# The first ten microseconds of an encoder layer: the norm's gain spread by TensorE, a new order of loads, casts and transposes

## The chip, the core and the metric

The kernel runs on one core of a Trainium2 chip. Its time is the device time of one execution in microseconds (us); the profile shows one execution, instruction by instruction. The engines are PE (TensorE), ACT (ScalarE), DVE (VectorE), POOL (GpSimd) and SP, which here only issues transfers. Each works through its own queue in order, and they wait for each other by semaphores.

## The reference

One residual layer on x, 1024 tokens of 1024 float32 numbers. Cut to what matters here:

```python
def rmsnorm(x, g):
    xf = x.astype(jnp.float32)
    y = xf * lax.rsqrt(jnp.mean(xf * xf, axis=-1, keepdims=True) + EPS)
    return (y * g.astype(jnp.float32)).astype(x.dtype)
...
h = rmsnorm(x, g_mix[l])
z = h @ w_in[l]                      # pooling channels | q | k | v
...                                  # pooling mixer and differential attention
gates = jax.nn.sigmoid(h @ w_gate[l] + b_gate[l])
merged = gates[..., :D] * (y_pool @ w_branch_pool[l]) + gates[..., D:] * (y_attn @ w_branch_attn[l])
x = x + merged @ w_out[l]
h2 = rmsnorm(x, g_ffn[l])
x = x + jnp.square(jax.nn.relu(h2 @ w_up[l])) @ w_down[l]
```

## The kernel before

Tokens lie in eight tiles x0 to x7 of 128 rows. Products are made in float32 by three matmuls (`mm3`, L123): each operand is split into a high part, rounded to the fast float32r, and a low part, the rest; hi times hi, hi times lo and lo times hi are summed in PSUM. `split` (L118) makes the parts: ACT casts the high one, DVE or POOL subtracts it for the low one.

`norm_transpose` (L262) turns a tile of x into normalised, transposed, split operands hT: a sum of squares by ACT (`ss`; for x0 ACT and DVE take half each), the factor rs by DVE and a power on POOL (L260, L275), hn = x * rs * g on DVE in two halves (L281), eight 128x128 transposes on PE into two PSUM banks hps (L286), then four casts and four subtractions to hT, one pair for each of four pieces of the depth (kp 0 to 3). g must lie in all 128 partitions: `gmb` is loaded by one DMA that reads the row 128 times (L370).

The weights of head 0 come in four pieces w0 to w3, each two DMAs of 192 KB into `rqkv` (L334) and two splits into `wqkv` (L354). `stage_qkv` multiplies: for a tile t, z is summed over eight k, and k = 2 kp and 2 kp + 1 use piece kp of hT and of the weights (L439). The string START sets the order of this opening; a token "xN" loads a tile, "nN" normalises it, "wN" loads a weight piece, "sN" splits it, and an "s" with a letter behind takes POOL for the low half instead of DVE. NX says at which step of the loop over head and tile the other tiles are normalised.

What each engine's queue looks like is decided by a scheduler that takes the instructions in the order of writing as priority and places each where its own timing model has it ready. It does so over the whole program, so a change at the start can move instructions far behind it.

Behind the opening come eight heads of attention, with the gate products and the pooling mixer as filling between them, then the projections, and an MLP whose two products are made of seven half-size products each (a Strassen-Winograd scheme): in `up_pair` (L1054), X, Y, Z and W are banks, A.. and AS1 to AS4 the split weight sides, B.. and BT1 to BT4 the split token sides, U2 and U3 copies of bank X between the products that are added to it, z5 a copy of Z.

Of the kernel before, what the change touches and what calls it, by code (L numbers as in the profile page):

```python
# [41 lines left out]

START = "x0 g n0 w0 w1 w2u w3u x1 s0p s1 x2 s2p s3 x3"
NX = [-2, -1, 0, 0, 0, 1, 2, 3]
LX = [-2, -2, -2, -2, 0, 0, 1, 1]
# [12 lines left out]
def encoder_kernel(  # L58
# [41 lines left out]

    hcount = [0]

    def htile(shape, dt, name, th):
# [14 lines left out]
    def split(hi, lo, src, lo_eng=None):  # L118

        nc.scalar.copy(hi, src)  # L120
        (lo_eng or nc.vector).tensor_tensor(lo, src, f(hi), op=ALU.subtract)  # L121

    def mm3(ps, lhs_hi, lhs_lo, rhs_hi, rhs_lo, first, last, more=False):  # L123

        kw = {"skip_group_check": True} if more else {}
        nc.tensor.matmul(ps, lhs_hi, rhs_hi, start=first, stop=False, **kw)  # L126
        nc.tensor.matmul(ps, lhs_hi, rhs_lo, start=False, stop=False, **kw)  # L127
        nc.tensor.matmul(ps, lhs_lo, rhs_hi, start=False, stop=last, **kw)  # L128

# [132 lines left out]
    def norm_transpose(xt, gb, t, dst, hn, small, banks, halves=False):  # L262
# [16 lines left out]
        for j in range(2):  # L279
            js = slice(j * 512, (j + 1) * 512)  # L280
            nc.vector.scalar_tensor_tensor(hn[:, js], xt[:, js], rs, gb[:, js], op0=ALU.mult, op1=ALU.mult)  # L281
            trp, trtag = banks[j % len(banks)]
# [17 lines left out]
    with ExitStack() as ph:  # L300
# [8 lines left out]

        xs = {}  # L310

# [8 lines left out]
        def load_x(t):  # L320
            xs[t] = ut([P, D], F32, f"x{t}")
            for c in range(0, D, 512 if t == 0 else D):
                e = c + 512 if t == 0 else D
                nc.sync.dma_start(xs[t][:, c:e], x[t * P : (t + 1) * P, c:e])

# [14 lines left out]
        def norm_x(t):  # L340
# [18 lines left out]
        for w in START.split():  # L359
            if w[0] == "x":  # L360
                load_x(int(w[1]))
            elif w[0] == "n":
                norm_x(int(w[1]))
            elif w[0] == "w":
                load_w(0, int(w[1]), utf if w[2:] else raw)
            elif w[0] == "s":
                split_w(0, int(w[1]), nc.gpsimd if w[2:] else nc.vector)
            elif w[0] == "g":
                gmb = ut([P, D], F32, "gmb")
                nc.sync.dma_start(gmb, g_mix[0].partition_broadcast(P))  # L370


        rows = sp.tile([32, P], F32, name="rows")
        nc.gpsimd.memset(rows, 0.0)
        nc.sync.dma_start(rows[0:16, :], b_gate[0].rearrange("(r p) -> r p", p=P))
# [6 lines left out]
        lqk = s1([P, 4, HD], F32, "lqk", "oq")  # L382
        nc.sync.dma_start(lqk, lambda_qk[0].partition_broadcast(P))

        dist = s1([P, S], F32, "dist", "dist")
# [44 lines left out]
        def stage_qkv(h, t):  # L430
# [4 lines left out]
            for k in range(NK):  # L435
                l_hi = hT[k // 2, th, 0][:, k % 2, c0 : c0 + P]
                l_lo = hT[k // 2, th, 1][:, k % 2, c0 : c0 + P]
                w = Wh[h][k]
                mm3(z[:, 0:384], l_hi, l_lo, w[:, 0, :], w[:, 1, :], k == 0, k == NK - 1)  # L439
                yield  # L440
# [191 lines left out]
        def stage(w, g):  # L632
# [19 lines left out]
            elif w == "W" and t == 0 and h:  # L652
                for kp in range(NK // 2):
                    load_w(h, kp)
                    split_w(h, kp, nc.gpsimd)

        for g in range(-2, N + 8):
# [3 lines left out]
            for t in range(1, NT):  # L661
                if NX[t] == g:
                    norm_x(t)
            if g == G_DIST:
# [103 lines left out]
    gate_units = gates()  # L768
    for _ in range(G_FIRST):
        next(gate_units)  # L770
# [565 lines left out]
```

## Time and profile before

| | |
|---|---|
| median of 3 runs | 1549.46 us (1548.1 to 1549.97) |
| the profiled execution | 1548.34 us |
| its span, first to last instruction | 1546.6 us |
| PE busy | 1526.0 us, 99% |
| DVE, ACT, POOL busy | 1012.4, 816.5, 350.9 us |
| first instruction on PE | 8.94 us |

A row of the timeline reads: start, duration (both us), engine, line of the kernel, operation, output<-input, partitions x elements, count; in brackets the idle time of the engine ahead of it and what ended that. "SPq" rows are issues of DMAs, not their transfers.

### The profile page before, as it was taken

The numbers are of one execution on the slowest core, as the hardware profiler recorded it, in microseconds if no ns is written. First come the engines' busy times: TensorE is split into PE (matmuls) and PEld (weight loads), VectorE is DVE, ScalarE is ACT, GpSimd is POOL, SyncE is SP. The second block draws the span as 40 slices with busy tenths as digits, with TensorE's granted clock in tenths as the row PEclk, the third lists the DMA queues.
The fourth block names the chain that finished last, engine by engine and source line by source line (L and its number), as shares of the span: only waits on it lengthen the run. The fifth ranks groups of instructions, "written<-read, shape, count | busy, mean of one in ns | idle before, by whom it ended". The sixth has DMA issues, their size and how long they took to land.

```text
span 1546.6 us, 22053 instructions
## 1 busy us (share of the span) xinstructions
PE 1526.0 (99%) x7649; PEld 1320.4 (85%) x7649; DVE 1012.4 (65%) x2268; ACT 816.5 (53%) x1808; POOL 350.9 (23%) x448
## 2 busy tenths in 40 slices
PE   7999999999999999999999999999999999999999
PEld 6899999999998989888888887888888788888887
DVE  7777777777878787865322448766666668556672
ACT  6656555666666565566432546565555634333331
POOL 6433334243525262315443400000000000000000
PEclk9999999999999999999999999999999999999999
DMA  7111212020202031547426534555432789537650
GB/s 230 49 54 48 64 39 73 20 79 32 81 28 84 28 96 42 177 132 250 139 93 205 177 105 124 180 172 176 137 136 109 259 312 389 196 123 256 225 192 28
DMA packets 166681, 206.41 MB, mean 133 GB/s; under 512 B 10069, under 2 KB 102954, under 8 KB 166570
## 3 DMA queue, kind: packets, MB, share of 16 engines
q1 hardware_dynamic: 149162, 177.71, 34.8%
q10 hardware_dynamic: 17408, 27.30, 4.7%
q8 instruction: 60, 0.98, 0.3%
q14 instruction: 51, 0.42, 0.1%
HBM read 150.42 MB, written 54.56 MB: 133 GB/s over the span
## 4 chain that ended last, share of the span: by engine, by line
PE 91%; DVE 3%; issue 2%; ACT 1%; DMA 1%; POOL 1%; SPq 1%; POOLq 0%; DVEq 0%; ACTq 0%
PE z L126 5%; PE z L128 5%; PE z L127 5%; PE Da L126 4%; PE Da L127 4%; PE Da L128 4%; PE g L126 3%; PE g L127 3%; PE g L128 3%; PE Db L126 3%; PE Db L127 3%; PE Db L128 3%; PE X L126 2%; PE X L128 2%; PE X L127 2%; PE sc L512 2%
## 5 line engine op out<-in xcount | busy, mean ns | idle before, releaser
L126 PE MATMUL z<-wqkv,hT 128*128 128x384 f32 x512 | 174.5, 341 | 0.4 <-DVE qn L453 0.3
L128 PE MATMUL z<-wqkv,hT 128*128 128x384 f32 x512 | 174.1, 340 | 0.0
L127 PE MATMUL z<-wqkv,hT 128*128 128x384 f32 x512 | 173.8, 339 | 0.0
L522 ACT ACTIVATE s<-s,nm 128x256 f32<-128x256 f32 (+7 forms) x128 | 99.6, 778 | 45.8 <-DVE nm L514 42.7
L260 POOL TENSOR_TENSOR ms<-ms,mhalf 128x4 f32<-128x4 f32 x64 | 66.5, 1039 | 158.0 <-DVE ms L259 136.7
L126 PE MATMUL g<-hT,fwgate 128*128 128x512 f32 x256 | 101.0, 395 | 0.1
L127 PE MATMUL g<-hT,fwgate 128*128 128x512 f32 x256 | 101.0, 395 | 0.0
L128 PE MATMUL g<-hT,fwgate 128*128 128x512 f32 x256 | 101.0, 395 | 0.0
L126 PEld LDWEIGHTS z<-wqkv,hT 128*128 128x128 f32 x512 | 96.8, 189 | 3.9 <-DVE qn L453 1.0
L127 PEld LDWEIGHTS z<-wqkv,hT 128*128 128x128 f32 x512 | 96.6, 189 | 3.0
L128 PEld LDWEIGHTS z<-wqkv,hT 128*128 128x128 f32 x512 | 96.6, 189 | 2.2 <-DVE hT L121 0.5
L514 DVE CUSTOM_DVE_ANT_0 s<-sc,dist 128x512 f32<-128x512 f32 (+3 forms) x128 | 74.7, 586 | 19.7 <-PE sc L512 18.2
L121 POOL TENSOR_TENSOR wqkv<-rqkv,wqkv 128x384 fp32r<-128x384 f32 x60 | 64.0, 1085 | 19.2 <-ACT wqkv L120 15.5
L121 DVE TENSOR_TENSOR AS<-s,AS 128x512 fp32r<-128x512 f32 x64 | 43.9, 688 | 35.8 <-ACT AS L120 35.6
L511 PE MATMUL sc<-K,Q 128*128 128x512 f32 (+2 forms) x192 | 66.6, 353 | 0.1
L512 PE MATMUL sc<-K,Q 128*128 128x512 f32 (+2 forms) x192 | 66.5, 354 | 0.0
L459 POOL TENSOR_TENSOR qn<-qn,ggh 128x128 f32<-128x128 f32 x64 | 32.3, 505 | 138.7 <-DVE qn L453 127.7
L485 ACT CAST Q<-tk 64x128 fp32r<-64x128 f32 x128 | 33.2, 259 | 57.8 <-DVE Q L484 56.0
L482 ACT CAST Q<-tk 64x128 fp32r<-64x128 f32 x128 | 33.0, 258 | 53.7 <-DVE K L481 52.3
L121 POOL TENSOR_TENSOR fwgate<-frgate,fwgate 128x512 fp32r<-128x512 f32 x32 | 44.5, 1394 | 51.9 <-ACT fwgate L120 51.8
L128 PEld LDWEIGHTS g<-hT,fwgate 128*128 128x128 f32 x256 | 48.1, 188 | 8.6
L126 PEld LDWEIGHTS g<-hT,fwgate 128*128 128x128 f32 x256 | 48.2, 188 | 7.3 <-ACT go L757 0.4
(430 smaller groups left out, 4640.7 us busy)
## 6 DMA issues: line engine op xcount, KB each, us to landing
wd<-in_w_down_dram SPq DMA_DIRECT2D x56, 512.0 KB, 5.3
wu<-in_w_up_dram SPq DMA_DIRECT2D x32, 512.0 KB, 4.5
udS<-us SPq DMA_DIRECT2D x64, 256.0 KB, 2.4
ur<-udS SPq DMA_DIRECT2D x32, 512.0 KB, 3.3
rqkv<-in_w_in_dram SPq DMA_DIRECT2D x64, 192.0 KB, 2.7
ud<-u ACTq DMA_DIRECT2D x48, 256.0 KB, 2.1
ur<-ud SPq DMA_DIRECT2D x24, 512.0 KB, 4.7
frgate<-in_w_gate_dram SPq DMA_DIRECT2D x32, 256.0 KB, 2.6
```

Of the source, the lines that this page charges most:

```text
L121: (lo_eng or nc.vector).tensor_tensor(lo, src, f(hi), op=ALU.subtract)
L126: nc.tensor.matmul(ps, lhs_hi, rhs_hi, start=first, stop=False, **kw)
L127: nc.tensor.matmul(ps, lhs_hi, rhs_lo, start=False, stop=False, **kw)
L128: nc.tensor.matmul(ps, lhs_lo, rhs_hi, start=False, stop=last, **kw)
L260: nc.gpsimd.tensor_tensor(dst, dst, mhalf[:, :n], op=ALU.pow)
L459: nc.gpsimd.tensor_tensor(qn[:, 2:4, :], qn[:, 2:4, :], ggh.unsqueeze(1).broadcast_to([P, 2, HD]), op=ALU.mult)
L482: nc.scalar.copy(q_hi, q)
L485: nc.scalar.copy(Q[other, m, 1, :], q)
L511: nc.tensor.matmul(dst, Q[:, i, 0, :], rhs, start=True, stop=False)
L512: nc.tensor.matmul(dst, Q[:, i, 1, :], rhs, start=False, stop=True)
L514: nc.vector.tensor_tensor_reduce(out=s[i][:, c : c + w], in0=sc[:, 0:w], in1=dist[:, o0 + c : o0 + c + w], scale=2.0 ** -(h + 1), scalar=B ...
L522: nc.scalar.activation(s[i][:, 0:n], s[i][:, 0:n], AF.Exp, bias=last, scale=-1.0, accum_out=Z[:, i, t : t + 1])
```

## The change

The gain g is loaded as one row of 4 KB by ACT's DMA queue; two matmuls with a row of ones spread it over 128 partitions into two PSUM banks (g_ps), from which hn of x0 is made directly. DVE copies the banks to gmb for the other tiles, behind the first low half of hT. All other loads stay on SP: x0, w0, w1, x1, w2, w3, then the other tiles; the small parameters are held behind the last of the first x loads, as are the weights of head 1 and the first gate weights. The splits of w1, w2, w3 are held behind the first cast of hT, and the low halves of w0, w1 and w2 are made by POOL, those of w3 by DVE (before: w0 and w2 by POOL, w1 and w3 by DVE). x1 is normalised behind the whole first product, and x2 to x5 are normalised from step 1 on.

```diff
-START = "x0 g n0 w0 w1 w2u w3u x1 s0p s1 x2 s2p s3 x3"
-NX = [-2, -1, 0, 0, 0, 1, 2, 3]
+START = "x0 g n0 w0 w1 x1 w2u w3u s0p s1p s2p x2 s3 x3"
+NX = [-2, 1, 1, 1, 1, 1, 2, 3]
...
-            nc.vector.scalar_tensor_tensor(hn[:, js], xt[:, js], rs, gb[:, js], op0=ALU.mult, op1=ALU.mult)
+            nc.vector.scalar_tensor_tensor(hn[:, js], xt[:, js], rs, gb[j], op0=ALU.mult, op1=ALU.mult)
...
+                if kp == 0:
+                    marks["hT"], marks["hTl"] = marks["hi"], marks["lo"]
...
-            norm_transpose(xs.pop(t), gmb, t, hT, hn, sp, banks, t == 0)
+            gb = g_ps if t == 0 else [gmb[:, 0:512], gmb[:, 512:D]]
+            norm_transpose(xs.pop(t), gb, t, hT, hn, sp, banks, t == 0)
+            if t == 0:
+                with tc.issue_after(marks["hTl"]):
+                    for j in range(2):
+                        nc.vector.tensor_copy(gmb[:, j * 512 : (j + 1) * 512], g_ps[j])
...
             elif w[0] == "s":
-                split_w(0, int(w[1]), nc.gpsimd if w[2:] else nc.vector)
+                with ExitStack() as behind:
+                    if w[1] != "0":
+                        behind.enter_context(tc.issue_after(marks["hT"]))
+                    split_w(0, int(w[1]), nc.gpsimd if w[2:] else nc.vector)
             elif w[0] == "g":
                 gmb = ut([P, D], F32, "gmb")
-                nc.sync.dma_start(gmb, g_mix[0].partition_broadcast(P))
+                g_row = ut([1, D], F32, "g_row")
+                issued["g"] = nc.scalar.dma_start(g_row, g_mix).ins
+                g_ps = [pool.tile([P, 512], F32, tag=tag, name=f"g_ps{tag}") for pool, tag in ((ps_o, "o"), (ps_f, "f"))]
+                for j, ps in enumerate(g_ps):
+                    nc.tensor.matmul(ps, f(ones)[0:1, :], g_row[:, j * 512 : (j + 1) * 512], start=True, stop=True)
...
+                    with ExitStack() as behind:
+                        if t == 1:
+                            behind.enter_context(tc.issue_after(marks["z"]))
+                        norm_x(t)
```

POOL's queue at the start, before: the factor of x0, the low halves of the first and third weight piece (`wqkv0_4` is k = 4, piece 2), then the factors of x1 and x2.

```order
L275 TENSOR_TENSOR rs0_157<-rs0_157,mhalf_98 128x1
L121 TENSOR_TENSOR wqkv0_0_197<-rqkv0_0_183,wqkv0_0_197 128x384
L121 TENSOR_TENSOR wqkv0_1_200<-rqkv0_0_183,wqkv0_1_200 128x384
L121 TENSOR_TENSOR wqkv0_4_211<-rqkv0_2_189,wqkv0_4_211 128x384
L121 TENSOR_TENSOR wqkv0_5_214<-rqkv0_2_189,wqkv0_5_214 128x384
L260 TENSOR_TENSOR rs1_247<-rs1_247,mhalf_98 128x1
```

The same place now:

```order
L276 TENSOR_TENSOR rs0_162<-rs0_162,mhalf_98 128x1
L122 TENSOR_TENSOR wqkv0_0_204<-rqkv0_0_190,wqkv0_0_204 128x384
L122 TENSOR_TENSOR wqkv0_1_207<-rqkv0_0_190,wqkv0_1_207 128x384
L122 TENSOR_TENSOR wqkv0_2_210<-rqkv0_1_193,wqkv0_2_210 128x384
L122 TENSOR_TENSOR wqkv0_3_213<-rqkv0_1_193,wqkv0_3_213 128x384
L261 TENSOR_TENSOR rs1_295<-rs1_295,mhalf_98 128x1
L122 TENSOR_TENSOR wqkv0_4_216<-rqkv0_2_198,wqkv0_4_216 128x384
L122 TENSOR_TENSOR wqkv0_5_219<-rqkv0_2_198,wqkv0_5_219 128x384
```

The second piece's two halves came in between, and the third piece's now stand behind the factor of x1.

ACT's queue around the end of the first product z0_0, before (hn1, hn2, ... are the squares of x1, x2, ...; hps1_0 and hps1_1 the transposed halves of x1; sq0_0 and V0_0 read the product):

```order
L277 ACTIVATE hn2_275,ss2_276<-x2_209 128x1024
L448 ACTIVATE sq0_0_428<-z0_0_369 128x256
L120 CAST hT0_0_0_147<-hps1_0_252 128x2x128
L120 CAST hT2_0_0_151<-hps1_1_262 128x2x128
L277 ACTIVATE hn3_301,ss3_302<-x3_223 128x1024
L120 CAST hT1_0_0_149<-hps1_0_252 128x2x128
L277 ACTIVATE hn4_335,ss4_336<-x4_271 128x1024
L120 CAST V0_0_365<-z0_0_369 128x128
```

And now:

```order
L278 ACTIVATE hn2_319,ss2_320<-x2_222 128x1024
L468 ACTIVATE sq0_0_435<-z0_0_264 128x256
L121 CAST hT0_0_0_152<-hps1_0_300 128x2x128
L121 CAST hT2_0_0_156<-hps1_1_310 128x2x128
L278 ACTIVATE hn3_345,ss3_346<-x3_230 128x1024
L426 ACTIVATE ls_245<-ls_245 128x2
L278 ACTIVATE hn4_379,ss4_380<-x4_252 128x1024
L121 CAST V0_0_260<-z0_0_264 128x128
L121 CAST hT1_0_0_154<-hps1_0_300 128x2x128
```

The cast of the second piece of x1 (hT1) moved behind ls, the squares of x4 and V.

From about the 130th matmul, and the 50th instruction of the other queues, both programs agree, up to one stretch at the start of the MLP, where some 50 instructions of PE, ACT and DVE are permuted. There, ACT's queue before (u11_3, AS3_0 and A22_0 belong to different pairs of columns, 3 and 0):

```order
L120 CAST BT4h_10414<-y7_10307 128x4x128
L120 CAST AS3_0_10848<-s3_0_10808 128x512
L120 CAST A22_0_10871<-wu0_1_10629 128x512
L120 CAST AS4_0_10892<-s4_0_10809 128x512
L1094 COPY U2_0_10827<-X0_10590 128x512
L1099 COPY z5_0_10845<-Z0_10829 128x512
L1074 ACTIVATE u11_3_10777<-u11_3_10777 128x512
```

And now:

```order
L121 CAST BT4h_10421<-y7_10314 128x4x128
L1102 ACTIVATE u11_3_10784<-u11_3_10784 128x512
L1103 ACTIVATE u11_3_10784<-u11_3_10784 128x512
L1107 DMA ud11_1_10424<-u11_3_10784 128x512
L1122 COPY U2_0_10834<-X0_10597 128x512
L1127 COPY z5_0_10852<-Z0_10836 128x512
L121 CAST AS3_0_10855<-s3_0_10815 128x512
L121 CAST A22_0_10878<-wu0_1_10636 128x512
```

The copies of X0 and Z0 now stand ahead of the casts. On PE, the second product added to X0 (with AS3) before came behind the end of Y3 and the twelve matmuls of W0; now it follows the product with AS2 at once:

```order
L129 MATMUL X0_10597<-BT2h_10413,AS2_0_10819 128x512
L127 MATMUL X0_10597<-BT3h_10417,AS3_0_10855 128x512
L128 MATMUL X0_10597<-BT3l_10418,AS3_0_10855 128x512
L127 MATMUL W0_10877<-BT4h_10421,A22_0_10878 128x512
L128 MATMUL W0_10877<-BT4l_10422,A22_0_10878 128x512
```

W0's first two matmuls stand inside that product, its other ten behind the next one's start.

More of the change, by code (lines that the diff above doesn't have):

```diff
@@ L101, in encoder_kernel @@
     hcount = [0]
+    marks = {}
     def htile(shape, dt, name, th):
@@ L127, in mm3 @@
         nc.tensor.matmul(ps, lhs_hi, rhs_lo, start=False, stop=False, **kw)
-        nc.tensor.matmul(ps, lhs_lo, rhs_hi, start=False, stop=last, **kw)
+        return nc.tensor.matmul(ps, lhs_lo, rhs_hi, start=False, stop=last, **kw).ins
     wcount = [0]
@@ L308, in s1 @@
             return sq_pool.tile(shape, dt, tag=tag, name=name, bufs=bufs)
-        xs = {}
+        xs, issued = {}, {}
         def utf(shape, name):
@@ L383, in encoder_kernel @@
         nc.sync.dma_start(lqk, lambda_qk[0].partition_broadcast(P))
+        late.close()
         dist = s1([P, S], F32, "dist", "dist")
@@ L653, in stage @@
                 for kp in range(NK // 2):
-                    load_w(h, kp)
+                    with ExitStack() as behind:
+                        if h == 1:
+                            behind.enter_context(tc.issue_after(started))
+                        load_w(h, kp)
                     split_w(h, kp, nc.gpsimd)
@@ L662, in encoder_kernel @@
                 if NX[t] == g:
-                    norm_x(t)
+                    with ExitStack() as behind:
+                        if t == 1:
+                            behind.enter_context(tc.issue_after(marks["z"]))
+                        norm_x(t)
             if g == G_DIST:
@@ L768, in encoder_kernel @@
     gate_units = gates()
-    for _ in range(G_FIRST):
+    with tc.issue_after(started):
+        next(gate_units)
+    for _ in range(G_FIRST - 1):
         next(gate_units)
```

16 lines of the change are left out of this document (10 added, 6 removed).

## The prediction

> **What bounds the kernel now.** I read the page first, then the waits of TensorE, then the first 30 us of the timeline engine by engine, and last the stretch near 957 us, the only other place where the new order differs.
>
> ```profile
> span 1546.6 us, 22053 instructions
> PE 1526.0 (99%) x7649; PEld 1320.4 (85%) x7649; DVE 1012.4 (65%) x2268; ACT 816.5 (53%) x1808; POOL 350.9 (23%) x448
> PE hps L286 <- DVE hn L281: 9.6, 2, 8.9
> ```
>
> TensorE is busy for all but 20.6 us of the span, and 9.6 of those are two waits for the normalised row hn, 8.9 of them before its first instruction. Every later stage is a TensorE queue that the other engines keep fed, so what the change gains or loses ahead of the point where both orders meet is simply carried to the end. The profiled execution took 1548.34 us, the median is 1549.46; I sum against the first and add the result to the second. The three times shown span 1.9 us, and about 0.2% (3.1 us) is what a measurement of this kernel can tell from no change.
>
> How the first 9 us are made:
>
> ```profile
> 0.73 1.28 ACT L269 ACT_TABLE_LOAD   x1 [0.73 <-PEq L1322]
> 0.74 0.87 SPq L324 DMA_DIRECT2D x<-in_x_dram  x2
> 1.65 0.42 SPq L370 DMA_DIRECT2D gmb<-in_g_mix_dram  x1
> 2.12 6.96 SPq L334 DMA_DIRECT2D rqkv<-in_w_in_dram  x8
> 3.41 0.63 ACT L269 ACTIVATE hn<-x 128x512 f32<-128x512 f32 x1 [1.39 <-DMA x<-in_x_dram]
> 5.29 0.56 POOL L275 TENSOR_TENSOR rs<-rs,mhalf 128x1 f32<-128x1 f32 x1 [3.03 <-DVE rs L274]
> 8.13 1.41 DVE L281 SCALAR_TENSOR_TENSOR hn<-x,rs,gmb 128x512 f32<-128x512 f32 x2 [3.00 <-DMA gmb<-in_g_mix_dram]
> 8.94 1.97 PE L286 MATMUL hps<-identf,hn 128*128 128x128 f32 x8 [8.94 <-DVE hn L281]
> ```
>
> The row factor rs is ready at 5.29 + 0.56 = 5.85, yet hn starts at 8.13: the broadcast load of g ends that wait. The weights are queued behind it on SP.
>
> **Term 1: the first transposes.** The load of 128 copies of g is replaced by one row on ACT's queue and two matmuls. The row's issue stands ahead of the table load, which ended at 2.01 while ACT waited until 3.41, so it costs nothing with 1.4 us of cover. I let the row land no later than the first half of x0, which is 64 times its size and was used at 3.41. The two matmuls are of a kind the trace lacks (fp32, not a transpose, 512 columns). From below:
>
> ```profile
> 10.59 0.69 PE L126 MATMUL z<-wqkv,hT 128*128 128x384 f32 x1
> 13.01 0.52 PE L127 MATMUL z<-wqkv,hT 128*128 128x384 f32 x1
> 13.33 0.47 PE L128 MATMUL z<-wqkv,hT 128*128 128x384 f32 x1
> 13.64 0.34 PE L126 MATMUL z<-wqkv,hT 128*128 128x384 f32 x1
> 13.82 0.34 PE L127 MATMUL z<-wqkv,hT 128*128 128x384 f32 x1
> ```
>
> 384 columns step by 0.32 us (13.01 to 13.33), so 512 cost 0.43; from above, the eight fp32 transposes of 128 columns take 10.59 - 8.94 = 1.65, or 0.21 each, so 512 cost 0.83. I take the second, the nearer in type: both banks are there at 3.41 + 1.66 = 5.1, before rs. Then hn starts at 5.9 instead of 8.13 and the transposes at 6.65 instead of 8.94: **2.3 us earlier**. [...]
>
> The loads, too, must be there:
>
> ```profile
> 10.00:20.00 10.00, 9.37 (x47) 8.08 (x45) 8.39 (x20) 8.07 (x20) 6.91 (x9) 1.00 0.95 318
> ```
>
> The last number is GB/s. At 318, from 3.41 on, the other half of x0 and piece 0 (0.66 MB) take 2.1 us, piece 1 and x1 (0.92 MB) 2.9 more: piece 0 is there at 5.5, x1 at 8.4, each before it is wanted below (5.85 and 10.1).
>
> The two copies of g into gmb on VectorE (by the 0.70 of an hn half, at most 1.4 us) stand where two weight subtractions stood, and lie under POOL's next step.
>
> **Term 2: the first product waits for POOL.** The change hands POOL the low halves of weight piece 1, too: six subtractions instead of four, with rs1 behind the fourth. Their prices:
>
> ```profile
> 9.21 5.09 POOL L121 TENSOR_TENSOR wqkv<-rqkv,wqkv 128x384 fp32r<-128x384 f32 x4 [3.36 <-DMA rqkv<-in_w_in_dram]
> L121 POOL TENSOR_TENSOR wqkv<-rqkv,wqkv x60: 1001/1019/1497, 9.2 to 553.9; 128x384 fp32r<-128x384 f32 x60
> 10.43 0.98 ACT L120 CAST wqkv<-rqkv 128x384 fp32r<-128x384 f32 x2
> 19.66 0.36 ACT L120 CAST hT<-hps 128x256 fp32r<-128x256 f32 x1
> 18.61 1.06 ACT L277 ACTIVATE hn<-x 128x1024 f32<-128x1024 f32 x1
> ```
>
> At this place one took 5.09 / 4 = 1.27; the best of all 60 took 1.00. With 1.27: piece 0 is done at 5.85 + 2.54 = 8.4. Piece 1's casts stand on ACT behind the first hT cast, which four transposes (0.83) release near 7.6; so hT ends at 8.0, the casts (0.49 each) at 8.5 and 9.0, POOL's fourth at 8.5 + 2.54 = 11.0. ACT goes on with three hT casts (to 10.1) and the squares of x1, 1.05 with their sum, to 11.3 with the hand-over; VectorE's step and rs1 (0.56) end near 12.1. Piece 2 follows on POOL: 12.1 + 2.54 = 14.65. From there the first product lacks eight matmuls at 0.18: it ends near 16.05. Before:
>
> ```profile
> 16.11 0.34 PE L128 MATMUL z<-wqkv,hT 128*128 128x384 f32 x1
> 16.54 0.36 ACT L448 ACTIVATE sq<-z 128x256 f32<-128x256 f32 x1
> 17.07 1.23 PE L286 MATMUL hps<-identf,hn 128*128 128x128 f32 x8 [0.63 <-DVE hn L281]
> 17.74 0.37 ACT L120 CAST hT<-hps 128x256 fp32r<-128x256 f32 x1 [0.84 <-PE hps L286]
> ```
>
> There it ended at 16.11 + 0.18 = 16.29. So of 2.3 us 0.24 are left. TensorE then waited 0.78 for hn of x1; now that is ready at 12.1 + 1.41 = 13.5 and the wait goes: transposes at 16.1 instead of 17.07, **1.0 us ahead**.
>
> **Term 3: ACT's queue behind it.** The new order puts the squares of x3 and x4, ls and V ahead of the second hT cast of x1; before, only the squares of x3 stood there.
>
> ```profile
> 20.55 0.41 DVE L121 TENSOR_TENSOR hT<-hps,hT 128x256 fp32r<-128x256 f32 x1
> 21.02 0.44 PE L128 MATMUL z<-wqkv,hT 128*128 128x384 f32 x1
> 21.07 0.25 ACT L120 CAST V<-z 128x128 fp32r<-128x128 f32 x1
> 21.35 0.29 DVE L121 TENSOR_TENSOR V<-z,V 128x128 fp32r<-128x128 f32 x1
> 21.48 0.21 ACT L406 ACTIVATE ls<-ls 128x2 f32<-128x2 f32 x1
> ```
>
> First hT cast: 0.67 after the transposes start, as before: 16.77. From there to the squares 18.61 - 17.74 = 0.87, so they start at 17.64; two of 1.05 and ls 0.21 end at 19.95, V's cast lets go near 20.15, the wanted cast ends at 20.5, V's low half (0.29) and this one (0.41) on VectorE at 21.2. The matmul that used it at 21.02 runs at 21.27: **0.25 us behind**. With POOL at 1.00 everything after it is some 0.5 earlier: 0.25 ahead. The same happens once more: the second casts of x2 now stand behind the squares of the second product, and the transposes of x4 need that bank. I give it 0.5, between 0 (VectorE's hn is early) and 1.05 (one such pair of casts behind one square). Afterwards TensorE is full.
>
> **Term 4: near 957 us.** Here the scheduler moved the W0 product out from between two products into bank X0.
>
> ```profile
> 956.88 0.62 ACT L120 CAST AS<-s 128x512 fp32r<-128x512 f32 x1 [1.48 <-DVE s L866]
> 958.45 0.58 ACT L1094 COPY U<-X 128x512 f32<-128x512 f32 x1
> 958.93 0.59 ACT L1099 COPY z<-Z 128x512 f32<-128x512 f32 x1
> 956.90 0.39 PE L128 MATMUL Y<-B21h,A 128*128 128x512 f32 x1
> 958.07 0.50 PE L126 MATMUL W<-BT4h,A 128*128 128x512 f32 x1 [0.79 <-ACT A L120]
> 958.41 0.40 PE L127 MATMUL W<-BT4l,A 128*128 128x512 f32 x1
> 958.88 0.50 PE L128 MATMUL W<-BT4h,A 128*128 128x512 f32 x1
> ```
>
> Before, TensorE lost 958.07 - 957.13 = 0.94 here and 0.24 more at 958.88. Now the same count of matmuls ends at 957.13, but the next one needs AS3, whose cast stands on ACT behind the copies U2 and z5, and U2 waits for that very end (957.3): U2, z5 and the cast at 0.5, 0.5 and 0.62 end at 958.95. TensorE loses 1.9 instead of 1.2: **0.7 behind**; 0 if the transfers ahead of it come otherwise, 0.95 without the second gap.
>
> **Sum.** 0.25 + 0.5 + 0.7 = 1.45 us later: 1549.8 for the profiled execution, 1550.9 for the median; its own range, with the ends above and 0.5 for the measurement, is 1548.7 to 1552.2. The banks lent to g are copied out near 10, and the next to want one is the first gate product, 19 us later; the other waits for the attention, later still:
>
> ```profile
> 28.91 0.39 PE L126 MATMUL g<-hT,fwgate 128*128 128x512 f32 x1
> ```
>
> **Rivals.**
> - *The early start goes through.* If POOL and ACT kept up, the first product would end 4.2 us (24 matmuls at 0.18) after starting at 10.59 - 2.3 = 8.3, at 12.6 instead of 16.29; with the 0.78 that is 4.5 ahead, less term 4: 1545.7. For it: all the weights are in SBUF sooner. Against it: six subtractions at the best 1.00 and rs1 already reach past 12.6. Chance 0.06.
> - *The clock falls back (slower).* Before, the step went from 0.32 to 0.18 at 13.64, 4.7 us after TensorE began, and there was one gap of 0.78. Now TensorE would be half idle from 9 to 15, with single matmuls between 11.3 and 14.6. If that resets the clock, the rows after the first product step by 0.32 for another 4.7 us: 4.7 x (1 - 0.18 / 0.32) = 2.06 us on top, 1553.0. It decides if steps of 0.32 stand after 16 us. [...] Chance 0.12.
> - *g isn't early.* Loads of 4 KB rows from r_dram, of another form, took this long:
>
> ```profile
> DMA to landing us min/median/max: 3.3/3.6/6.2
> ```
>
> At 6.2 the row lands at 6.9, the first bank is there at 7.8, hn and all that hangs on it come 1.9 later than in term 1: 1552.8. For it: ACT's queue has carried nothing before in this run. Against it: x0's first half, on an equally fresh queue, took 2.7. Chance 0.06.
>
> **Numbers.** Forecast 0.75: 1550.9. The range reaches down past the forecast's end by the spread of the times and up to the clock rival: 1547.3 to 1553.3. Faster by over 0.2%: the first rival and a little for what I overlook, 0.07. Slower by over 0.2%: the clock rival and the late row, less than their sum since each only just passes the bound, 0.17. Within: 0.76.
>
> **What would show it.** Right: first transposes at 6.5 to 7, gaps of TensorE before the second matmul of pieces 1 and 2 that end on POOL wqkv, no gap ahead of the transposes of x1, and an idle of nearly 2 us near 958 that ends on ACT AS. Wrong: POOL done with piece 2 before 13.5; steps of 0.32 after 16 us; first transposes after 7.5.

## The result, and the profile after

The changed kernel takes 1552.02 us (median of 19 runs, 1550.71 to 1554.01) against 1549.62 for the one before; the ratio is 1.0017 (95% interval 1.001 to 1.0025). So it is slower by 2.4 us (0.17%), just within the 0.2% that the prediction took as its bound. One of the 19 runs of the kernel before took 8785.71 us, and the ratio leaves it out. The profiled execution took 1550.72 us, 2.4 more than the 1548.34 of before. Its span is 1548.9 us.

TensorE's waits (engine, operation and line, what it waited for; us in total, times, longest):

```profile
PE g_pso L386 <- POOL edge L900: 2.3, 1, 2.3
PE X L127 <- ACT AS L121: 2.1, 1, 2.1
...
PE z L128 <- POOL wqkv L122: 1.6, 2, 0.9
...
PE hps L287 <- DVE hn L282: 1.0, 2, 0.7
```

The 9.6 us of waiting for hn are down to 1.0. Yet the kernel ends later. Three waits are new beside the first: for POOL's low halves of weights, for ScalarE's cast of a weight piece (at 12.47 below), and one of 2.1 us for the cast AS. The first two lie in the first product; here are TensorE's rows from its first matmul to the transposes of x1:

```profile
2.26 2.04 PE L386 MATMUL g_pso<-g_row,ones 1*128 1x512 f32 x2 [2.26 <-POOL edge L900]
4.10 1.91 PE L386 MATMUL g_psf<-g_row,ones 1*128 1x512 f32 x2
6.73 1.97 PE L287 MATMUL hps<-identf,hn 128*128 128x128 f32 x8 [0.72 <-DVE hn L282]
...
12.47 0.45 PE L127 MATMUL z<-wqkv,hT 128*128 128x384 f32 x1 [0.39 <-ACT wqkv L121]
13.86 0.44 PE L128 MATMUL z<-wqkv,hT 128*128 128x384 f32 x1 [0.94 <-POOL wqkv L122]
...
15.27 0.69 PE L128 MATMUL z<-wqkv,hT 128*128 128x384 f32 x1 [0.61 <-POOL wqkv L122]
15.75 0.52 PE L129 MATMUL z<-wqkv,hT 128*128 128x384 f32 x1
...
17.73 0.52 PE L129 MATMUL z<-wqkv,hT 128*128 128x384 f32 x1
18.05 1.14 PE L287 MATMUL hps<-identf,hn 128*128 128x128 f32 x8
```

The transposes of x0 start at 6.73 instead of 8.94. Those of x1 start at 18.05 instead of 17.07: in this pair of profiles the whole lead of 2.2 us is lost inside one product, and 1.0 more. From 15.75 to 17.73 the matmuls step by 0.32 us (16.07, 16.39 and so on to 17.73): the slow step has come back after it had already been at 0.18, and the granted clock from 15.27 to 18.05 was 0.50, where it was 1.00 from 9 to 12 us.

The other engines in that stretch:

```profile
10.60 0.37 ACT L121 CAST hT<-hps 128x256 fp32r<-128x256 f32 x1 [0.98 <-DVE hT L122]
10.87 1.06 ACT L278 ACTIVATE hn<-x 128x1024 f32<-128x1024 f32 x1
...
12.29 0.55 POOL L261 TENSOR_TENSOR rs<-rs,mhalf 128x1 f32<-128x1 f32 x1 [1.56 <-DVE rs L260]
12.81 2.40 POOL L122 TENSOR_TENSOR wqkv<-rqkv,wqkv 128x384 fp32r<-128x384 f32 x2
...
8.63 0.68 DVE L356 COPY gmb<-g_pso 128x512 f32<-128x512 f32 x1
...
12.88 2.88 DVE L282 SCALAR_TENSOR_TENSOR hn<-x,rs,gmb 128x512 f32<-128x512 f32 x2 [0.67 <-POOL rs L261]
```

POOL stands idle for 1.56 us ahead of rs1, with piece 2's low halves queued behind it: it is not POOL's speed that is late there but the squares of x1 on ScalarE, at 10.87. They stand behind the fourth cast of hT at 10.60, which waited 0.98 us for VectorE, and VectorE copied g from 8.63 on, in two copies, the second to 9.90.

And near 958 us, on VectorE and ScalarE and then TensorE:

```profile
956.02 0.69 DVE L894 TENSOR_TENSOR y<-y 128x512 f32<-128x512 f32 x1 [2.45 <-DMA y<-nd]
956.63 0.69 DVE L891 TENSOR_TENSOR u<-Y,x 128x512 f32<-128x512 f32 x1
...
958.13 0.69 DVE L894 TENSOR_TENSOR s<-wu,wu 128x512 f32<-128x512 f32 x1
...
959.05 0.59 ACT L1122 COPY U<-X 128x512 f32<-128x512 f32 x1 [0.40 <-ACT u L1103]
959.53 0.59 ACT L1127 COPY z<-Z 128x512 f32<-128x512 f32 x1
960.01 0.63 ACT L121 CAST AS<-s 128x512 fp32r<-128x512 f32 x1
...
958.18 0.39 PE L129 MATMUL X<-BT2h,AS 128*128 128x512 f32 x1
960.69 0.50 PE L127 MATMUL X<-BT3h,AS 128*128 128x512 f32 x1 [2.13 <-ACT AS L121]
```

On ScalarE the two copies stand ahead of the cast, as the order showed. On VectorE the reload of y came late (a wait of 2.45 us), and the sum for S3, from which the cast is made, stands behind it.

To split the loss between the two places, take one row that every kernel has: the transposes `ta` of the first head, whose wait ends near 124 us. From there on the programs are the same until the MLP's first products.

```profile
123.83 0.63 PE L567 MATMUL ta<-identf,s 128*128 128x128 f32 x4 [0.59 <-DVE AT_4l L121]
```

```profile
125.24 0.63 PE L587 MATMUL ta<-identf,s 128*128 128x128 f32 x4 [0.59 <-DVE AT_4l L122]
...
1544.73 0.39 PE L129 MATMUL Da<-w_7h,u_7l 128*128 128x512 f32 x1
```

The start lost 125.24 - 123.83 = 1.41 us. The rest lost 0.96: 1419.49 from this row to the last matmul, where before it was 1418.53 (the last one at 1542.36). The figure for the rest repeats better than the one for the start: the experiments hold a second profile of the old opening, word for word the same up to the MLP, and there `ta` stands at 124.53, and a second profile of the changed kernel has it at 125.62.

### The profile page after: what moved, and what is told of

Same layout as the page of the kernel before. It is cut to its first block, busy times and chain, and to the rows that moved or that the text cites. A ratio compares the mean times of both kernels' runs of the same rounds, so it can differ in the third digit from the quotient of the medians.

```text
span 1548.9 us, 22074 instructions
## 1 busy us (share of the span) xinstructions
PE 1531.4 (99%) x7653; PEld 1322.6 (85%) x7653; DVE 1015.2 (66%) x2268; ACT 816.6 (53%) x1808; POOL 352.5 (23%) x450
## 4 chain that ended last, share of the span: by engine, by line
PE 91%; DVE 3%; issue 2%; DMA 2%; ACT 1%; POOL 1%; SPq 0%; POOLq 0%; ACTq 0%; DVEq 0%
PE z L127 5%; PE z L129 5%; PE z L128 5%; PE Da L127 4%; PE Da L128 4%; PE Da L129 4%; PE g L127 4%; PE g L129 4%; PE g L128 4%; PE Db L127 3%; PE Db L128 3%; PE Db L129 3%; PE X L127 2%; PE X L129 2%; PE X L128 2%; PE sc L531 2%
## 5 line engine op out<-in xcount | busy, mean ns | idle before, releaser
L122 POOL TENSOR_TENSOR wqkv<-rqkv,wqkv 128x384 fp32r<-128x384 f32 x62 | 65.3, 1071 | 15.7 <-ACT wqkv L121 15.3
```

Of the source, the lines that this page charges most:

```text
L122: marks["lo"] = (lo_eng or nc.vector).tensor_tensor(lo, src, f(hi), op=ALU.subtract).ins
```

## Experiments

All changes start from the changed kernel unless said otherwise. "x1" is the start of the transposes of x1, "ta" the row above, "rest" the time from it to the last matmul, and "slow" about how many matmuls behind 940 us stepped by 0.43 us where others take 0.23. The runs were made in four rounds, on more than one chip, and in each the kernel before ran beside them: "beside" is its median there, and the ratio, with its 95% interval, is to it. Medians of different rounds are best compared by how far they stand above "beside".

| kernel | median us | beside | ratio | x1 | ta | rest | slow |
|---|---|---|---|---|---|---|---|
| before | 1549.62 | | | 17.07 | 123.83 | 1418.53 | 0 |
| changed | 1552.02 | 1549.62 | 1.0017 (1.001 to 1.0025) | 18.05 | 125.24 | 1419.49 | 0 |
| changed, once more | 1552.50 | 1548.87 | 1.0019 (1.001 to 1.0028) | 18.42 | 125.62 | 1419.68 | 0 |
| old start, new order at 957 | 1550.81 | 1549.20 | 1.0012 (1.0003 to 1.0021) | 18.20 | 124.53 | 1419.57 | 0 |
| ScalarE's order at 957 set back | 1551.39 | 1549.31 | 1.0016 (1.0008 to 1.0025) | 18.04 | 125.58 | 1419.88 | 0 |
| and VectorE's | 1551.26 | 1549.20 | 1.0015 (1.0006 to 1.0024) | 17.96 | 125.62 | 1420.76 | 13 |
| copies of g later | 1552.32 | 1549.31 | 1.0019 (1.001 to 1.0028) | 18.04 | 125.90 | 1420.71 | 6 |
| spare matmuls in the start | 1550.71 | 1549.31 | 1.001 (1.0001 to 1.0019) | 17.25 | 124.89 | 1420.75 | 8 |
| and at 946 | 1551.70 | 1549.20 | 1.0014 (1.0005 to 1.0023) | 17.24 | 124.34 | 1421.06 | 8 |
| piece 1 back on VectorE | 1551.20 | 1549.31 | 1.0013 (1.0004 to 1.0022) | 16.79 | 124.48 | 1420.74 | 9 |
| and lambda later | 1556.99 | 1549.20 | 1.0054 (1.004 to 1.0068) | 18.12 | | | |
| g alone, on the kernel before | 1552.67 | 1548.87 | 1.0023 (1.0014 to 1.0032) | 18.02 | 126.09 | 1420.75 | 8 |
| both repairs | 1549.63 | 1548.87 | 1.0004 (0.9995 to 1.0013) | 16.85 | 124.83 | 1419.31 | 6 |
| both, with spare matmuls | 1549.42 | 1548.87 | 1.0002 (0.9993 to 1.0011) | 16.94 | 124.15 | 1418.96 | 0 |

### The start: whose queue, and the clock

**Piece 1's low halves back on VectorE.**

```diff
-START = "x0 g n0 w0 w1 x1 w2u w3u s0p s1p s2p x2 s3 x3"
+START = "x0 g n0 w0 w1 x1 w2u w3u s0p s1 s2p x2 s3 x3"
```

> The changed kernel with one part undone: the two low halves of weight piece 1 are subtracted on VectorE again, so POOL has four subtractions, not six, ahead of the end of the first product; TensorE's order is unchanged. Theory (POOL's row of six is what ends the first product): POOL starts piece 2 behind rs1 and is done with it about 1 us sooner or more, no wait of TensorE on POOL inside piece 2 above 0.5 us, the median 0.5 to 2 us under the changed kernel's. Rival (ScalarE sets rs1, and VectorE's longer row, with its two more subtractions ahead of hT's low halves, makes ScalarE's casts later by as much): rs1 at 12 or later, POOL done with piece 2 at 14.7 or later, time within 0.4 us of the changed kernel's or above it.

```profile
11.80 0.55 POOL L261 TENSOR_TENSOR rs<-rs,mhalf 128x1 f32<-128x1 f32 x1 [3.83 <-DVE rs L260]
...
18.10 0.29 DVE L424 TENSOR_TENSOR lp<-lqk 128x128 f32<-128x128 f32 x1 [1.15 <-DMA lqk<-in_lambda_qk_dram]
...
16.79 1.04 PE L287 MATMUL hps<-identf,hn 128*128 128x128 f32 x8
...
19.49 0.45 PE L129 MATMUL z<-wqkv,hT 128*128 128x384 f32 x1 [1.02 <-DVE hT L122]
```

With two subtractions fewer POOL only waits longer for rs1 (3.83 us instead of 1.56), and rs1 comes 0.49 earlier. So the row of six is not the limit, as this run's theory had it; rs1, ahead of piece 2 on the same queue, is. (ScalarE's fourth cast of hT now stands behind the squares of x1, which start at 9.77, 1.10 earlier; but VectorE has its low halves ahead of the step to rs1, which starts at 11.58 instead of 12.05.) The transposes of x1 come 1.26 earlier all the same: 0.49 from rs1, the rest because no slow stretch follows (the steps stay at 0.18). Then a new wait shows: VectorE's step lp waits 1.15 us for the load of lqk, which the change put behind the first loads of x and w, and the low half of hT that TensorE wants stands behind lp. At `ta` 0.76 of the 1.26 is left.

**Spare matmuls in TensorE's waits.** They write a PSUM bank that nothing reads; the computation is otherwise whole.

```diff
+FILL = {3: 2, 4: 5, 5: 3}
...
+                    nc.tensor.matmul(z[:, 0:384], l_hi, w[:, 0, :], start=k == 0, stop=False)
+                    for _ in range(fill):
+                        nc.tensor.matmul(spare[:, 0:384], l_hi, w[:, 0, :], start=True, stop=True)
```

> The changed kernel with ten more matmuls of 384 columns into a PSUM bank that nothing reads: two inside weight piece 1 and five and three behind the first matmul of the two halves of piece 2, that is in TensorE's own waits for POOL. They add some 0.2 us of work at most to the path. Theory (the waits let TensorE's clock fall back, and the steps of 0.32 us from 15.3 to 18 are the price): no step of 0.32 from 13 us on, transposes of x1 near 16.9 instead of 18.05, the median about 1.2 us (1.0 to 2.0) under the changed kernel's and the runs closer together than its 1550.7 to 1554.0. Rival (the clock falls back for another reason, such as the kind of work ahead, or its steps cost nothing since POOL sets the end): the same transposes at 17.9 to 18.3 and the same time within 0.3 us.

No row of 0.32 stands behind 10 us, x1's transposes come at 17.25, and the median falls to 1550.71, 1.3 under the changed kernel's, or 1.0 if each is counted from the kernel before of its round. The two intervals still overlap, but the profiles show what moved: with TensorE's waits filled the clock stays up, and x1's transposes come 0.8 earlier. The table by stage (stretch, its length, TensorE's busy time and matmuls, granted clock, DMA share, GB/s) has it as granted clock, in the changed kernel and then here:

```profile
0.00:30.00 30.00, 24.48 (x104) 0.94 0.73 244
```

```profile
0.00:30.00 30.00, 24.54 (x116) 1.00 0.74 244
```

The same stretch has 0.94 in the second profile of the changed kernel and in the three runs with copies of g later, ScalarE's order set back, and VectorE's too; it has 1.00 with the waits filled at 946 as well, with piece 1 back on VectorE, and in both versions with both repairs. Without the fall `ta` stands at 124.15 to 124.89 (five profiles, three of them with piece 1 back on VectorE), with it at 125.24 to 125.90 (five). So the slow clock is a cause of the loss, not only a mark of it. Here only part of the gain reaches `ta` (0.35 of 0.80), because the wait behind lp appears too. The runs did not close up (1549.86 to 1552.25); why is seen further on, in eight rows of 0.43 (948.30 to 951.68, 3.4 us):

```profile
948.30 0.63 PE L128 MATMUL Y<-B21h,A 128*128 128x512 f32 x1
948.73 0.63 PE L129 MATMUL Y<-B21l,A 128*128 128x512 f32 x1
...
951.68 0.39 PE L130 MATMUL Y<-B21h,A 128*128 128x512 f32 x1
```

**The copies of g behind all low halves of hT.**

```diff
-                with tc.issue_after(marks["hTl"]):
+                with tc.issue_after(marks["lo"]):
```

> The changed kernel; the two copies of g into gmb on VectorE stand behind the last low half of hT of x0 instead of behind the first. Theory (the copies are not hidden: ScalarE's fourth hT cast waits 0.98 us at 10.60 for a low half that stands behind them, and the squares of x1, the casts of weight piece 2, rs1 and POOL's piece 2 all stand behind that cast): squares of x1 from about 9.9 instead of 10.87, rs1 near 11.3 instead of 12.29, POOL done with piece 2 near 14.2 instead of 15.2, transposes of x1 near 17.0 instead of 18.05, the median 0.5 to 1.5 us under the changed kernel's. Rival (as predicted, the copies lie under POOL's four subtractions and cost nothing): rs1 stays at 12.2 or later and the time stays within 0.3 us.

```profile
10.45 1.06 ACT L278 ACTIVATE hn<-x 128x1024 f32<-128x1024 f32 x1
...
10.93 0.68 DVE L356 COPY gmb<-g_pso 128x512 f32<-128x512 f32 x1
...
12.12 0.14 DVE L260 TENSOR_SCALAR rs<-ss 128x1 f32<-128x1 f32 x1
...
12.35 0.55 POOL L261 TENSOR_TENSOR rs<-rs,mhalf 128x1 f32<-128x1 f32 x1 [1.61 <-DVE rs L260]
```

A miss. The squares of x1 move from 10.87 to 10.45, but the two copies now stand on VectorE directly ahead of the step that makes rs1 from them; it starts at 12.12 instead of 12.05. The 1.19 us of copies lie on the way to rs1 in either place. What rs1 would do without them was not tried.

**The steps for lambda later**, on top of piece 1 back on VectorE.

```diff
+                    if t == 1:
+                        with tc.issue_after(marks["lo"]):
+                            lambdas()
```

> The kernel with piece 1's low halves back on VectorE (the run of that name), and beside it the steps for lambda (lp, ls) behind the low halves of hT of x1 on VectorE's queue. Theory (what took back the 1.2 us that the earlier end of the first product gave is VectorE's wait for the late load of lqk, 1.15 us at 18.1, with the low halves of hT behind it): transposes of x1 near 16.8 as there, first low half of hT of x1 near 17.8 instead of 19.02, no wait of TensorE on hT above 0.3 us, X0 starts 0.8 to 1.2 us sooner than that run's 926.33, so near 925.3. Rival (ScalarE's squares of x3 and x4 ahead of the next casts, term 3 as predicted, hold it all the same): the wait of about 1 us comes back at the next transposes or the second half of the second product, X0 at 926 or later.

Inconclusive: 1556.99. Moving these steps made the scheduler write another order for the whole first half, and new waits of 0.3 to 1.3 us stand between 277 and 646 us. At the place itself VectorE no longer waits for lqk, but a slow stretch stands at 15.8 to 17.8 and again from 20.15 (granted clock 0.89 in the first 30 us), so the start cannot be compared.

**g alone**, on the kernel before: only the row, the two matmuls and the copies; order of loads and casts as it was.

```diff
-                nc.sync.dma_start(gmb, g_mix[0].partition_broadcast(P))
+                g_row = ut([1, D], F32, "g_row")
+                issued["g"] = nc.scalar.dma_start(g_row, g_mix).ins
```

> The kernel before with one part of the change alone: g as a row on ScalarE's queue, spread by TensorE, with the copies into gmb; the order of loads, START and NX are those before. The scheduler's order near 957 us comes out as in the changed kernel. Theory (the early g is worth something only up to the next thing that the first product waits for, which is x1 behind all weight pieces and POOL's four subtractions): first four transposes at 6.7 instead of 8.9, transposes of x1 at 15.5 to 16.2 instead of 17.07, X0 0.5 to 1.5 us sooner than 925.66, given back by 1.0 near 957, the median within 0.7 us of before. Rival (nothing is gained, since hn's second half now stands on VectorE behind a low half of piece 1, which waits for its load): transposes of x1 at 17 or later and the median 1 us or more above before.

```profile
7.46 1.04 DVE L121 TENSOR_TENSOR wqkv<-rqkv,wqkv 128x384 fp32r<-128x384 f32 x1
8.42 0.73 DVE L281 SCALAR_TENSOR_TENSOR hn<-x,rs,g_psf 128x512 f32<-128x512 f32 x1
...
9.38 1.05 PE L286 MATMUL hps<-identf,hn 128*128 128x128 f32 x4
11.40 0.69 PE L128 MATMUL z<-wqkv,hT 128*128 128x384 f32 x1 [0.97 <-DVE hT L121]
```

The rival was right: hn's second half stands behind a low half of weights, the second four transposes come at 9.38, and TensorE begins early but thinly. Its matmuls stay at 0.32 a step until 17 us (17 rows from 11.89 to 17.01), and x1's transposes come at 18.02, no sooner than in the changed kernel. Here starting early was worth nothing, because the queue could not be kept full.

### The order near 957 us

**The new order on the old start.** One spare matmul ahead of Z0's first product, added to the kernel before, is enough to make the scheduler write TensorE's, ScalarE's and VectorE's rows there as in the changed kernel; the opening stays as it was.

```diff
+        for _ in range(busy):
+            nc.tensor.matmul(ps, Bq["11"][0][:, 0, 0:P], Bq["11"][0][:, 0, :], start=True, stop=True)
```

> The kernel before, with one matmul of 512 columns more into bank Z0 ahead of the first product that uses it (in a wait of 1.5 us, so it costs nothing itself). This one instruction makes the scheduler write the orders of TensorE, ScalarE and VectorE near 957 us as in the changed kernel; the opening is word for word the one before. Theory (the loss near 957 is the new order there, on whatever opening): X0 starts at 925.7 as before; idle of about 2 us near 959 on the cast AS; from the start of X0 to the last matmul 617.8 us where it was 616.7, the median 1.1 us (0.6 to 1.6) above that of before. Rival (the stall comes of where the opening leaves the transfers, not of the order): 616.7 and a median within 0.4 us of before.

```profile
960.27 0.50 PE L126 MATMUL X<-BT3h,AS 128*128 128x512 f32 x1 [2.18 <-ACT AS L120]
```

The same idle of 2.2 us, and 1419.57 us in the rest instead of 1418.53: 1.04 us, as in the changed kernel (0.96 and 1.15). The median is 1.2 above the before of the table and 1.6 above that of its round. The 1.04 is the loss by itself, and the start has no part in it. (X0 did not start at 925.7 as expected but at 926.52: `ta` is at 124.53 instead of 123.83, the old opening with a longer slow stretch, 14 rows from 12.42 to 16.58 instead of 8. So one and the same opening brings x1's transposes at 17.07 in one execution and at 18.20 in another.)

**ScalarE's rows set back, then VectorE's.** First the casts of AS3, A22 and AS4 ahead of U2 and z5 for pair 0, and W0's product back between the two into X0 (the part of the edit for the copies):

```diff
+            with tc.issue_after(marks["hi"]):
+                nc.scalar.copy(U2, X)
+                nc.scalar.copy(z5, Z)
```

> The changed kernel; near 957 us only the order is set back close to the one before: the casts of S3, A22 and S4 ahead of the copies U2 and z5, the product of A22 into W between the two products into X0. The start is the changed one. Theory (term 4: ScalarE's copies ahead of the cast of AS3 cost TensorE about 1 us, here the one new stall behind the start): no idle over 1.2 us on the cast AS near 958, the last matmul about 1.0 us nearer to where X0 starts, the median about 1.0 us under the changed kernel's, so some 1551.0 against 1552.0. Rival (the stall only takes the place of one that a transfer makes anyway, and the loss lies wholly in the start): another wait of the same length beside it, the time as the changed kernel's within 0.3 us.

```profile
960.68 0.50 PE L127 MATMUL W<-BT4h,A 128*128 128x512 f32 x1 [1.55 <-ACT A L121]
...
962.09 0.50 PE L129 MATMUL W<-BT4h,A 128*128 128x512 f32 x1 [0.67 <-DVE A L122]
```

The rival held: 1.55 + 0.67 in two waits instead of 2.13 in one, and nothing gained in the rest (1419.88). The median is 0.6 under the changed kernel's, 0.3 counted from before, well inside the intervals. The copies were not the only cause. The other is on VectorE, here in the kernel before:

```profile
954.05 0.69 DVE L866 TENSOR_TENSOR y<-y 128x512 f32<-128x512 f32 x1 [1.80 <-DMA y<-nd]
955.43 0.69 DVE L121 TENSOR_TENSOR BT4l<-y,BT4h 128x512 fp32r<-128x512 f32 x1 [0.69 <-ACT BT4h L120]
956.16 0.69 DVE L866 TENSOR_TENSOR s<-wu,wu 128x512 f32<-128x512 f32 x1
```

Before, y came at 954.05 and the sum for S3 2.11 behind it, at 956.16. In the changed kernel they stand at 956.02 and 958.13, again 2.11 apart: the addition u at 956.63 only fills the 0.69 in which VectorE waited for BT4's cast. But both are 1.97 later. Of this, 1.30 is the later start of X0 (926.96 for 925.66), and 0.67 comes of the other u, which moved ahead of B22's low half (951.67 and 952.27; before it stood behind, B22's at 950.36 and u at 950.97): the reload of y overwrites B22's source and is issued when that low half ends (at 951.12 before and 953.02 now). The next kernel sets both u's back too:

```diff
+        if p in (2, 3):
+            with tc.issue_after(marks["lo"]):
+                next(pairs[p])
```

> The kernel with ScalarE's casts of AS3, A22 and AS4 ahead of U2 and z5 (the run of that name), and beside it on VectorE the two additions that finish u11 of pairs 2 and 3 behind the low half of B22 and of BT4 instead of ahead of them. Theory (what kept the stall near 959 alive there is VectorE: u ahead of B22's low half delays the reload of y by 0.6 us, and u ahead of BT4's low half the sums for S3 by 0.6 more): y lands about 0.6 nearer to the start of X0, idle on A and AS near 958 together 1.0 to 1.6 us instead of 2.2, from X0 to the last matmul about 617.2 us where that run had 618.1. Rival (ScalarE's row alone, or the transfer itself, sets it): still 2 us of idle.

No wait above 0.15 us stands near 959, but the profile has 13 slow rows from 948.84 on, which give the casts 2.6 us to catch up, so this run alone proves nothing. The kernel with both repairs and spare matmuls, below, shows this order without a slow stretch.

### The clock behind 945 us, and a better version

Two waits of 1.5 and 0.8 us, 1.3 us apart, stand near 946 in every kernel without spare matmuls there, before included. Here they are in the changed kernel:

```profile
946.28 0.50 PE L127 MATMUL Z<-BT1h,AS 128*128 128x512 f32 x1 [1.50 <-ACT BT1h L121]
947.60 0.50 PE L127 MATMUL Y<-B21h,A 128*128 128x512 f32 x1 [0.83 <-DVE u L891]
```

In six of these eleven profiles a slow stretch of 6 to 13 rows follows; in five none does. The table by stage has the granted clock there, 1.00 in the changed kernel and 0.97 in the one with piece 1 back on VectorE:

```profile
925.00:985.00 60.00, 55.53 (x249) 1.00 0.47 144
```

```profile
925.00:985.00 60.00, 56.01 (x245) 0.97 0.46 141
```

**Spare matmuls at 946 as well** as in the start:

```diff
-        u_product(Z, "5", a_op(p, "S1", S1, dve))
+        u_product(Z, "5", a_op(p, "S1", S1, dve), 0 if p else 7)
```

> The changed kernel with the ten spare matmuls in the first product (as in the run with those alone) and seven more of 512 columns into bank Z0 ahead of its first product, in the wait of 1.5 us near 946. Theory (the runs of one kernel spread over 2 to 3 us because TensorE's clock falls back for some 3.4 us in some executions, behind 945 us as in three of the five profiles of changed kernels, and at 15 us): no row of 0.4 us and more a step behind 945 us and none of 0.32 behind 13 us, the runs within about 1.2 us of each other, none above 1551.3, median near 1550.2. Rival (the spread has another source, such as DMA): rows of 0.43 stand behind 946 in spite of the filler, or the runs spread over more than 2 us as before.

```profile
959.94 0.74 PE L128 MATMUL X<-BT3h,AS 128*128 128x512 f32 x1 [2.15 <-ACT AS L122]
960.48 0.63 PE L129 MATMUL X<-BT3l,AS 128*128 128x512 f32 x1
```

Half a miss: no slow rows behind 946, but now they stand behind the next wait, the new one at 959.94 (steps of 0.43 from 960.48 to 963.46), and the runs spread as before (1550.21 to 1552.67) around 1551.70, not 1550.2. The change has made a second place where they can stand.

**Both repairs** (piece 1 on VectorE, and the two queues near 957 set back), without and with spare matmuls in the start and at 946:

```diff
-START = "x0 g n0 w0 w1 x1 w2u w3u s0p s1p s2p x2 s3 x3"
+START = "x0 g n0 w0 w1 x1 w2u w3u s0p s1 s2p x2 s3 x3"
...
+            with tc.issue_after(marks["hi"]):
+                nc.scalar.copy(U2, X)
+                nc.scalar.copy(z5, Z)
...
+            with tc.issue_after(marks["lo"]):
+                next(pairs[p])
```

> The changed kernel with both repairs: piece 1's low halves on VectorE, and near 957 us the order of the run with ScalarE's and VectorE's rows set back. Theory (the two losses add up: about 1.2 us of the start, of which 0.6 stays won by the run with the first repair, and 1.1 us near 957): X0 starts near 926.3; from there to the last matmul 616.5 to 617.2 us if the clock stays up; the median 1549.3 to 1550.3, within 0.5 us of before. Rival (the second repair only showed no stall because a slow clock stretch ahead of it let the casts catch up): idle of 1.5 us and more near 959 once that stretch is absent, and a median at 1551 or above.

The second one adds to this:

```diff
+FILL = {4: 3, 5: 3}
...
+        u_product(Z, "5", a_op(p, "S1", S1, dve), 0 if p else 7)
```

> The kernel of the other run with both repairs, and in it six spare matmuls in the waits of the first product and seven in the wait near 946. [...]

```profile
958.82 0.50 PE L128 MATMUL W<-BT4h,A 128*128 128x512 f32 x1 [1.21 <-ACT A L122]
```

1549.63 and 1549.42: in the same round the changed kernel took 1552.50 and the one before 1548.87. So 2.9 and 3.1 of 3.6 us are taken back, and both are the same as before as far as can be measured (both intervals hold 1, and the medians stand 0.8 and 0.6 above). All 22 runs lie below 1550.4, ten of the changed kernel's eleven above 1550.8. So the two places together account for nearly all of the loss. In detail not all went as expected: without spare matmuls X0 starts at 926.79 instead of 926.3. With them the median is 0.2 lower. At a granted clock of 1.00 (925 to 985 us) the wait near 959 is 1.21 us (before: 0.79 and 0.24), and the rest takes 1418.96 us, 0.43 above before: the repair takes back about 0.6 of the 1.0. The runs are closer together (1.2 and 1.7 us, where the changed kernel had 3.3), but as close without the spare matmuls as with them. What remains is not the clock's: with the spare matmuls the granted clock is 1.0 in all eleven runs, and they still lie 1.7 us apart. No version beats the kernel before.

**The changed kernel once more**, without an edit:

> The changed kernel itself once more, beside the others on the same chip. [...]

The profiled run took 1551.28, with the slow rows at 16.12 to 18.10, idle of 2.17 on AS at 961.37, and none slow behind 945. The first transposes came at 7.11 and those of x1 at 18.42, where the first profile has 6.73 and 18.05, so the start moves by 0.4 us between executions of one program. The eleven runs again fall into 1549.6 to 1551.7 and 1552.5 to 1552.9. Both profiles of this kernel are of the lower group. That the upper one has the slow stretch behind 945 too (about 1.25 us: rests of 1420.7 with it, 1419.5 without) is likely from its kin, and not shown by a profile of this kernel itself. The granted clock, on record for every run, speaks for it: of the first 19 runs the nine below 1552 us have 0.998 on average and the nine above 1552.4 have 0.997, and a granted clock of 0.50 (as from 15.27 to 18.05) for eight rows of 0.43, 3.4 of 1550 us, would be 0.001 less (an estimate).

## Why the prediction was right, and where it was not

The time (1550.9 forecast, 1552.02 measured) is within the range, the sign and the two places were right, and the loss is 2.4 where the sum said 1.45. That the start's part came out near is in part luck: the sum gave the loss to term 3, and the runs show it in the first product, much of it by the clock. By its steps:

- **Term 1 held.** First transposes at 6.73 (6.65 forecast), the second bank of g at 4.10 + 1.91 = 6.0 instead of 5.1: the first bank took 1.84 (2.26 to 4.10), not 0.83 (the wrong row was taken as the nearest). It cost nothing, as said; nor did it cost anything that piece 0 came later than 5.5 (ScalarE's casts of it waited until 5.98 and 6.82). The trace has two records for each of these matmuls, which start 0.85 to 0.99 apart.
- **Term 2 had the chain right and its size wrong.** Its sum led from ScalarE's casts and the squares of x1 over rs1 to POOL's piece 2, and so it was: the last two waits of the product (0.94 and 0.61) end on POOL. The reason in its heading was wrong: POOL's first four subtractions took 0.98 and 0.99 on average instead of 1.27, piece 1 was done at 10.72 (11.0 forecast), and POOL then idled; no wait on POOL stands inside piece 1, where a sign had one. What was late was rs1: 12.84 instead of 12.1, because ScalarE's fourth cast of hT waited 0.98 us for VectorE, which was busy with the copies of g. Those copies were priced at nothing, "under POOL's next step"; that is the step that failed, as the trace has it (the run that moved them only put them ahead of rs1 in another place). So piece 2 was done at 15.21 instead of 14.65, and the eight matmuls "at 0.18" then took 2.78 us (15.27 to 18.05) instead of 1.4. The two make up the 1.95 by which x1's transposes missed their 16.1.
- **The clock rival came about**, by its own test (steps of 0.32 after 16 us, at a granted clock of 0.50), and had 0.12. It was priced at 2.06 on top. About 8 rows at 0.32 instead of 0.18 are 1.1; filling the waits took 0.8 off x1's transposes and 1.0 to 1.3 off the median.
- **Term 3** had the lead of 1.0 at x1's transposes and 0.75 more lost behind them. There was no lead to lose: from these transposes to `ta` the changed kernel takes 107.2 us in both profiles, the old opening 106.8 and 106.3, so 0.4 to 0.9 are lost. Where the product did end early (piece 1 back on VectorE: 107.7), it was not ScalarE's squares that held the next one but VectorE's lp, waiting for lqk; what the change does to that load was left out.
- **Term 4**: 0.7 forecast, 0.96 to 1.15 measured, 1.04 on the old start. ScalarE's copies were only part of it: taking them out of the way gained nothing while the reload of y stayed late, and the u on VectorE that makes it late was overlooked.
- So the start cost 1.4 us in the first pair of profiles (0.7 to 1.8 over the two of each opening) where the sum had a net loss of 0.75, and the place at 957 1.0 where it had 0.7.

## What to carry to other kernels

A product that starts earlier than its operands can follow is spread thin, and here TensorE, busy for 1.25 of the 3.19 us from 12.08 to 15.27, then ran at a granted clock of 0.50 for 2.78: count what arrives in such a stretch, not only when the first matmul can go. When a scheduler decides, look for permutations far from the edit (here one more matmul in the program was enough to move 1 us), and read all engines' rows there, not just the one that the wait names. A wait named "POOL" may be for what POOL itself waits for.

## What the runs showed of the hardware

- **The clock fell behind stretches in which TensorE was partly busy.** Between 11.9 and 15.3 us TensorE of the changed kernel had waits of 0.39 + 0.94 + 0.61 = 1.94 us, began four matmuls (12.47, 13.86, 14.14, 14.32), and was slow from 15.3 to 18.1 (granted clock 0.50 from 15.27 to 18.05). The sum of the waits does not decide it alone: with 0.94 + 0.61 (ScalarE's order at 957 set back) the clock fell too, to 0.94 over the first 30 us; with 0.70 + 0.62 + 0.22 (both repairs) it was 1.00. Near 946, a slow stretch stands behind 1.5 + 0.8 us within 3 us in six of eleven profiles. A slow stretch lasts from 2.8 us (15.27 to 18.05) to about 4, in one profile 13 rows of 0.43, or 5.6; within one kernel it falls at another moment each time (rows of 0.32 from 16.12 to 18.10 and from 15.75 to 17.73). What sets its start and its length was not shown.
- **The granted clock shows falls, not the slow rows at the start.** It is 1.00 from 0 to 30 us in the run with g alone, with its 17 rows of 0.32 that no row of 0.18 precedes, and 0.94 in the changed kernel, whose rows of 0.32 from 15.75 to 17.73 stand behind rows of 0.18.
- **VectorE and POOL took longer side by side.** While POOL subtracted piece 2 (1.00 and 1.45 us; 1.00 each alone), the two halves of hn of x1 took 1.47 and 1.49 on VectorE, where one takes 0.75 otherwise (1.42 for both, before). A low half of hT, which reads one of its two operands from PSUM, took 0.41 beside POOL as ever (at 13.79 with piece 1 back on VectorE).
